# A two-part fp32 product: the context's high and low parts side by side in one 512-column matmul

## The chip, the cores and the metric

The kernel runs on one core of a Trainium2 chip, in one launch. The metric is its device time in microseconds, the median of repeated runs. Before the change three runs gave 1920.5, 1927.2 and 1932.17 us, so a median of 1927.2.

## The reference, cut to what matters

Two layers work on 512 latent tokens and 256 context tokens of width 1024. Layer 0 is grouped-query attention followed by a gated FFN of inner width 2816, layer 1 a bidirectional Mamba-2 (SSD) mixer followed by the same kind of FFN. The context passes through both mixers and the first FFN; only the latent stream is returned, so the second FFN has no context. All arithmetic is fp32.

```
for i in range(DEPTH):
    ...
    h_l = modulate(rms_norm(x, norm_mix_w[i]), mod_l[0], mod_l[1])
    h_c = modulate(rms_norm(ctx, norm_mix_w[i]), mod_c[0], mod_c[1])
    ...
    x = x + mod_l[2] * o_l
    if need_ctx_out:
        ctx = ctx + mod_c[2] * o_c
    h_l = modulate(rms_norm(x, norm_ffn_w[i]), mod_l[3], mod_l[4])
    x = x + mod_l[5] * conv_ffn(h_l, ffn_w_up[i], ffn_conv_w[i], ffn_conv_b[i], ffn_w_down[i])
    if need_ctx_out:
        h_c = modulate(rms_norm(ctx, norm_ffn_w[i]), mod_c[3], mod_c[4])
        ctx = ctx + mod_c[5] * conv_ffn(h_c, ffn_w_up[i], ffn_conv_w[i], ffn_conv_b[i], ffn_w_down[i])
```

`conv_ffn` splits `h @ w_up` into gate and value, convolves the gate over three neighbouring tokens, and multiplies `silu(gate) * value` by `w_down`.

## The kernel before

**Three products for one.** Activations lie transposed: channels on the 128 partitions, tokens along the free axis, 512 columns for the latent stream (L) and 256 for the context (C). TensorE takes a rounded fp32 format (fp32r), so every weight and every activation is split into a high part (a rounded copy, written by ACT) and a low part (the rest, a subtraction on DVE or POOL; `split`, line 81, and `modulated`, line 275). A product is three matmuls into one PSUM accumulation: high weights times high input (line 105), high weights times low input (106), low weights times high input (108). That is `mm3`, line 100. For the latent stream each of the three has 512 columns, for the context 256. Below, the three matmuls of one 128-row step for one stream are called a triple.

**Where the parts lie.** `htiles` (line 271) makes the high and the low tile of a stream separately, from a ring of 16 tiles per width. The FFN's hidden activations are split into two tiles of 768 columns (`hdh`, `hdl`, in `up`, line 841). The scratch ring t3 has 24 buffers of 768 columns during the first FFN.

**PSUM.** There are two buffers S of two banks (latents in columns 0 to 511, context in 512 to 767) and four buffers B of one bank.

**Layer 0, mixer.** `attention` (line 379) projects queries, keys and values. Context queries and keys come from six tiles `ps_c` and four tiles `ps_q`, eight triples each. The output projection runs in three groups of heads through `down` (`project`, line 1304, and the last group directly); its inputs are split in `osplit`.

**FFN.** `up` makes one 128-channel hidden tile: a gate tile and a value tile (`gemm_in`, line 351, eight steps, first 24 matmuls for one stream, then 24 for the other), ACT and DVE read the gate tile for the convolution and SiLU, DVE multiplies by the value tile and splits the result. There are 22 hidden tiles. After every two of them, `flush` runs `down` (line 779): for each of eight output tiles m it multiplies the two pending hidden tiles by `w_down` into a bank per stream, and DVE adds each bank, times a gate vector, into the residual (line 797). During the first FFN, DVE also computes the second layer's modulation in 96 pieces (`ada_dve`, line 154, instruction `junk`), taken from a generator a piece at a time between the tiles.

**Changeovers.** The last flush of a stage runs one segment after another: the context, then two halves of the latents. The norm of a segment runs beside the next segment's products. `first_tiles` (line 368) then makes the first two tiles of the next stage, starting with the context and the first half of the latents while the second half is still being normed.

**Layer 1, mixer.** `ssd` (line 889) makes a tile for the time steps (dt), and for each of eight groups two x tiles, one B tile, one C tile and two z tiles; x and B have both streams. `conv` (line 964) copies a tile out of PSUM with ACT into a row with gaps, then ACT and DVE run a five-tap convolution over it. The eight groups' states and outputs follow in `core`, one group behind. At the end the latent residual is loaded back from DRAM into `xn`, two tiles of 256 columns per m, and leaves at the end of the kernel in the same pieces.

**What sets the order.** The kernel is written for a planner that orders each engine's instructions at compile time: program order gives the priority, an instruction goes where its engine is free and its inputs are ready by the planner's own timing, and the planner assigns buffers as they fall free. So matmuls of a later tile can stand between those of an earlier one. Only the first part of `attention` fixes the order by hand for TensorE, ACT and DVE. On the chip each engine follows its list. Weights come through one DMA queue (SP) into tiles of 1024 columns (10 buffers) and are split by ACT and DVE (lines 85 and 87).

## Time and profile before

| | |
|---|---|
| median of three runs | 1927.2 us |
| runs | 1920.5, 1927.2, 1932.17 us |
| span of the profiled execution | 1929.7 us, mean granted clock of TensorE 0.990 |
| attention and output projection, about | 0 to 440 us |
| first FFN, about | 440 to 1000 us |
| SSD mixer, about | 1000 to 1550 us |
| second FFN, about | 1550 to 1930 us |

The profile is of one execution by the hardware profiler, and its own time is the span, from the first to the last instruction. It is 2.5 us above the median and within the range of the three runs. PE is TensorE's matmul, PEld its weight load, DVE VectorE, ACT ScalarE, POOL GpSimd, SP the engine that issues the DMAs. A row of the groups view names the kernel's line, the engine, the operation, what is written from what, the shape and the count; then the busy time in us, the mean length of one in ns, and the idle time before with what ended it. A row of the timeline gives the start in us, the length in us, and, in brackets, the idle time before it. A matmul's length includes its way through the pipeline, so two neighbours overlap, and what one costs is the distance from its start to the next one's. Some matmul records are missing, a few per cent at most.

### The profile page before, as it was taken

Reading aid. Unit: us, or ns where it says so; the run is one execution under the profiler, and the core shown is the slowest. Engines: PE = TensorE matmul, PEld = TensorE weight load, DVE = VectorE, ACT = ScalarE, POOL = GpSimd, SP = SyncE. Lnnn points to the kernel's source line nnn. Section 1 sums busy time; section 2 is a strip of 40 time slices with the busy share of each in tenths; the row PEclk is TensorE's granted clock in tenths of the full one; section 3 lists DMA queues with packets and bytes.
Section 4 is the critical chain, followed back from the end, with each engine's and each line's share of the span. In section 5 each row is a group of like instructions: output and inputs, shape, how many; then the busy total and the mean of one; then the engine's idle time right before and its main releaser. Section 6 shows DMA issues by size and latency. Waiting matters only on the chain.

```text
span 1929.7 us, 27392 instructions
## 1 busy us (share of the span) xinstructions
PE 1877.4 (97%) x10744; PEld 1533.9 (79%) x10744; DVE 1337.2 (69%) x1976; ACT 844.2 (44%) x1446; POOL 312.5 (16%) x274
## 2 busy tenths in 40 slices
PE   8989999999999999999999999999999999999999
PEld 6755544678888888888888888888888878888887
DVE  5577777768777777775577777777878466555555
ACT  3655444345222222222256777766677343333331
POOL 2241101022000000000031334443335210000000
PEclk9989998999999999999999999999999999999999
DMA  8221343104434443332222444344343322323332
GB/s 334 77 88 37 124 150 128 45 23 143 128 123 131 131 131 122 121 95 62 68 92 63 132 117 124 110 131 120 106 136 120 99 77 88 109 88 101 97 99 87
DMA packets 73424, 210.00 MB, mean 109 GB/s; under 512 B 8912, under 2 KB 14416, under 8 KB 73168
## 3 DMA queue, kind: packets, MB, share of 16 engines
q1 hardware_dynamic: 73296, 208.26, 34.0%
q8 instruction: 84, 1.38, 0.3%
q14 instruction: 44, 0.36, 0.1%
HBM read 198.79 MB, written 6.82 MB: 107 GB/s over the span
## 4 chain that ended last, share of the span: by engine, by line
PE 77%; DVE 8%; ACT 4%; issue 3%; POOL 2%; DMA 2%; SPq 0%; POOLq 0%; DVEq 0%; ACTq 0%
PE ps_up L108 10%; PE ps_up L106 10%; PE ps_up L105 10%; PE ps_d L105 6%; PE ps_d L106 6%; PE ps_d L108 6%; PE ps_in L108 4%; PE ps_in L106 4%; PE ps_in L105 4%; PE ps_o L650 2%; PE ps_s L686 2%; PE ps_st L1043 2%; PE ps_wo L108 1%; DVE ht L281 1%; PE ps_wo L105 1%
## 5 line engine op out<-in xcount | busy, mean ns | idle before, releaser
L87 DVE TENSOR_TENSOR wl<-wst,wh 128x1024 fp32r<-128x1024 f32 x205 | 255.4, 1246 | 222.8 <-PE ps_up L106 110.1
L85 ACT CAST wh<-wst 128x1024 fp32r<-128x1024 f32 x211 | 221.2, 1049 | 411.7 <-DMA wst<-in_wup 336.6
L106 PE MATMUL ps_up<-hlf,wh 128*128 128x512 f32 x1008 | 357.1, 354 | 0.0
L105 PE MATMUL ps_up<-hhf,wh 128*128 128x512 f32 x1008 | 356.9, 354 | 0.0
L108 PE MATMUL ps_up<-hhf,wl 128*128 128x512 f32 x1008 | 356.8, 354 | 0.0
L106 PEld LDWEIGHTS ps_up<-hlf,wh 128*128 128x128 f32 x1008 | 190.6, 189 | 26.2
L105 PEld LDWEIGHTS ps_up<-hhf,wh 128*128 128x128 f32 x1008 | 190.6, 189 | 26.2
L108 PEld LDWEIGHTS ps_up<-hhf,wl 128*128 128x128 f32 x1008 | 190.5, 189 | 25.9
L105 PE MATMUL ps_in<-hhs,wh 128*128 128x512 f32 (+1 forms) x560 | 204.4, 365 | 0.0
L106 PE MATMUL ps_in<-hls,wh 128*128 128x512 f32 (+1 forms) x560 | 199.4, 356 | 0.0
L108 PE MATMUL ps_in<-hhs,wl 128*128 128x512 f32 (+1 forms) x560 | 198.7, 355 | 0.0
L105 PE MATMUL ps_d<-hdh,wh 128*128 128x512 f32 (+1 forms) x568 | 193.7, 343 | 1.4 <-DVE X L797 1.2
L108 PE MATMUL ps_d<-hdh,wl 128*128 128x512 f32 (+1 forms) x568 | 193.4, 341 | 0.0
L106 PE MATMUL ps_d<-hdl,wh 128*128 128x512 f32 (+1 forms) x568 | 192.9, 340 | 0.3 <-DVE hdl L87 0.3
L797 DVE SCALAR_TENSOR_TENSOR X<-ps_d,mod,X 128x512 f32<-128x512 f32 (+1 forms) x240 | 132.9, 588 | 20.8 <-PE ps_d L108 20.4
L106 PEld LDWEIGHTS ps_d<-hdl,wh 128*128 128x128 f32 x568 | 106.7, 188 | 15.5 <-DVE hdl L87 0.7
L105 PEld LDWEIGHTS ps_d<-hdh,wh 128*128 128x128 f32 x568 | 106.3, 188 | 15.4 <-DVE X L797 1.7
L105 PEld LDWEIGHTS ps_in<-hhs,wh 128*128 128x128 f32 x560 | 105.9, 189 | 15.1 <-issue 1.2
L167 DVE SCALAR_TENSOR_TENSOR junk<-wada,cb 128x1024 f32<-128x1024 f32 x96 | 117.2, 1220 | 1.1 <-ACT cb L159 0.9
L108 PEld LDWEIGHTS ps_in<-hhs,wl 128*128 128x128 f32 x560 | 105.8, 189 | 14.7
L108 PEld LDWEIGHTS ps_d<-hdh,wl 128*128 128x128 f32 x568 | 106.7, 188 | 13.3
L106 PEld LDWEIGHTS ps_in<-hls,wh 128*128 128x128 f32 x560 | 106.0, 189 | 13.2
(344 smaller groups left out, 3525.0 us busy)
## 6 DMA issues: line engine op xcount, KB each, us to landing
wst<-in_wup SPq DMA_DIRECT2D x88, 512.0 KB, 3.6
wada<-in_adaT SPq DMA_DIRECT2D x48, 512.0 KB, 3.6
wst<-in_win SPq DMA_DIRECT2D x48, 512.0 KB, 3.6
wst<-in_wdown SPq DMA_DIRECT2D x44, 512.0 KB, 4.2
wada<-in_adaB SPq DMA_DIRECT2D x32, 512.0 KB, 5.2
E<-ad SPq DMA_DIRECT2D x64, 256.0 KB, 7.3
ec<-ead SPq DMA_DIRECT2D x64, 128.0 KB, 5.1
wst<-in_wout SPq DMA_DIRECT2D x16, 512.0 KB, 3.5
```

Of the source, the lines that this page charges most:

```text
L85: keep(nc.scalar.copy(hi, src))
L87: keep(eng.tensor_tensor(lo, src, _r(hi), ALU.subtract))
L105: mm(out, wh, ah, start=first, stop=False)
L106: mm(out, wh, al, start=False, stop=False)
L108: mm(out, wl, ah, start=False, stop=last)
L167: g.tc.keep_in_program_order(nc.vector.scalar_tensor_tensor(junk, w, 1.0, cb[:, v * D : (v + 1) * D], ALU.mult, ALU.mult, accum_out=md[:, ...
L281: nc.vector.scalar_tensor_tensor(t[:, c0:c1], ap, g.moda[layer][ca][:, m, v : v + 1], rs[:, c0:c1], ALU.mult, ALU.mult)
L650: nc.tensor.matmul(po[S64[e], :n], v, pr[:, 512 * e + off : 512 * e + off + n], start=first, stop=last)
L686: nc.tensor.matmul(outs[e], a[S64[e], k], b[S64[e], q], start=i == 0, stop=False)
L797: nc.vector.scalar_tensor_tensor(ap, o[:, c0:c1], gate[:, m, v : v + 1], ap, ALU.mult, ALU.add)
L1043: nc.tensor.matmul(ps[:, d * 256 : (d + 1) * 256], Bt[:, t * P : (t + 1) * P], xw[d][t], start=t == ts[0], stop=t == ts[-1])
```

## The change

The context's high and low parts move into one tile of two rows of 256 columns. One matmul of 512 columns multiplies both by the high weights, into a full bank: columns 0 to 255 hold high times high, 256 to 511 high times low. A second matmul of 256 columns adds the low weights times the high part to the first half. The latent triples stay as they are, except that the last step runs them in reverse order; where a group starts and stops in the same step with two halves, three narrow matmuls are kept. The two halves are added after the last step, in one of three ways:

- `fold`: ACT copies the second half to SBUF, DVE adds it into the first half in PSUM (up tiles of the FFN, the first tiles of a stage; of the SSD's two first tiles only the dt tile)
- `summed`: ACT copies the first half to its SBUF place, as before, and DVE adds the second half there (`ps_c`, `ps_q`, the x and B tiles of the SSD)
- in `down` the residual update on DVE runs once per half

The low and high hidden parts of the first FFN get tiles of two rows of 768 (`hd2`, six of them), and its scratch ring has 12 buffers instead of 24. `xn` becomes one tile of 512 columns per m, so its loads and the final stores are 8 transfers instead of 16.

```
     wh, wl = w
     mm = g.nc.tensor.matmul
-    for out, (ah, al) in outs:
-        mm(out, wh, ah, start=first, stop=False)
-        mm(out, wh, al, start=False, stop=False)
-    for out, (ah, al) in outs:
-        mm(out, wl, ah, start=False, stop=last)
+    for out, a in outs:
+        if len(a) == 3:
+            parts = [(out.rearrange("p (s n) -> p s n", s=2), wh, a[2]), (out[:, :C], wl, a[0])]
+        else:
+            parts = [(out, wh, a[0]), (out, wh, a[1]), (out, wl, a[0])]
+        if first and last and len(a) == 3:
+            mm(out[:, C:], wh, a[1], start=True, stop=True)
+            parts[0] = (out[:, :C], wh, a[0])
+        elif last:
+            parts.reverse()
+        for i, (o, s, mv) in enumerate(parts):
+            mm(o, s, mv, start=first and i == 0, stop=last and i == len(parts) - 1)
+
+
+def both(t):
+
+    return t[:, 0, L:], t[:, 1, L:], t[:, :, L:]
+
+
+def fold(g, ps):
+
+    t = t3(g, "fold", n=C)
+    g.nc.scalar.copy(t, ps[:, C : 2 * C])
+    g.nc.vector.tensor_tensor(ps[:, :C], ps[:, :C], t, ALU.add)
+
+
+def summed(g, out, ps):
+
+    g.nc.scalar.copy(out, ps[:, :C])
+    g.nc.vector.tensor_tensor(out, out, ps[:, C : 2 * C], ALU.add)
...
 def htiles(g, n, name):
+    if n == C:
+        t = g.p.tile([P, 2, C], F32R, tag="h256", bufs=8, name=f"h{name}")
+        return t[:, 0], t[:, 1], t
     return tuple(g.p.tile([P, n], F32R, tag=f"h{n}", bufs=16, name=f"{p}{name}") for p in ("hh", "hl"))
...
+                if k == KT - 1 and folded:
+                    for i, a, b in run:
+                        if i:
+                            fold(g, ps[:, off[i] : off[i] + 2 * C])
                 yield
...
+    if len(norm.streams) > 1:
+        for ps, _ in tiles[:folds]:
+            fold(g, ps[:, L:])
     return [ps for ps, _ in tiles]
...
-            k_step(k, j, ps[:, :C], hc)
-        nc.scalar.copy(raw[j][:, L:], ps[:, :C])
+            k_step(k, j, ps, hc)
+        summed(g, raw[j][:, L:], ps)
...
-                    nc.vector.scalar_tensor_tensor(ap, o[:, c0:c1], gate[:, m, v : v + 1], ap, ALU.mult, ALU.add)
+                    for h in range(2 if i else 1):
+                        nc.vector.scalar_tensor_tensor(ap, o[:, h * C + c0 : h * C + c1], gate[:, m, v : v + 1], ap,
+                                                       ALU.mult, ALU.add)
...
-        hi, lo = t3(g, "hdh", F32R, n=tot), t3(g, "hdl", F32R, n=tot)
-        split(g, hd, hi, lo)
...
+        hl = g.t3p.tile([P, 2, tot], F32R, tag="hd2", bufs=6, name="hd2")
+        split(g, hd, hl[:, 0], hl[:, 1])
+        return [(hl[:, 0, :L], hl[:, 1, :L]), both(hl)]
...
-            nc.scalar.copy(raw[:, L + 4 : L + 4 + C], ps[:, L:T])
+            summed(g, raw[:, L + 4 : L + 4 + C], ps[:, L:])
...
-    xn = [[g.p.tile([P, C], F32, tag="h256", bufs=16, name=f"x{m}{i}") for i in range(2)] for m in range(KT)]
+    xn = [[g.p.tile([P, L], F32, tag="h256", bufs=8, name=f"x{m}")] for m in range(KT)]
     for m in range(KT):
-        for i in range(2):
-            nc.sync.dma_start(xn[m][i], xd[m * P : (m + 1) * P, i * C : (i + 1) * C])
+        nc.sync.dma_start(xn[m][0], xd[m * P : (m + 1) * P])
...
-    g.t3p, g.n3 = pool("pf", phf), 24
+    g.t3p, g.n3 = pool("pf", phf), 12
```

More of the change, by code (lines that the diff above doesn't have):

```diff
@@ L283, in modulated @@
     bias = g.mod[layer][cb][:, m, v : v + 1]
-    hi, lo = (h[:, a:b] for h in hl)
+    hi, lo = (h[:, a:b] for h in hl[:2])
     if pool:
@@ L348, in gen, with gemm_in @@
             yield
-def gemm_in(g, tiles, h, off, segs):
+def gemm_in(g, tiles, h, off, segs, folded=True):
     for run in segs:
@@ L365, in firsts, with first_tiles @@
     return [load_w(g, u) for u in units]
-def first_tiles(g, ws, norm, bg):
+def first_tiles(g, ws, norm, bg, folds=2):
     ends = ending(norm.streams)
     tiles = [(S(g, "ps_first"), w) for w in ws]
-    for _ in gemm_in(g, tiles, norm.h, (0, L), [ends[:-1], ends[-1:]]):
+    for _ in gemm_in(g, tiles, norm.h, (0, L), [ends[:-1], ends[-1:]], False):
         next(bg, None)
@@ L513, in values @@
                 w = tuple(w[:, (k % 4) * 256 : (k % 4 + 1) * 256] for w in wv[k // 4])
-                ah, al = (a[:, c0 : c0 + P] for a in h[k])
+                ah, al = (a[:, c0 : c0 + P] for a in h[k][:2])
                 for i, (s, mv) in enumerate(((ah, w[0]), (ah, w[1]), (al, w[0]))):
@@ L858, in up @@
             nc.vector.tensor_tensor(hd[:, a:b], cv[:, a:b], ps, ALU.mult)
-        hi, lo = t3(g, "hdh", F32R, n=tot), t3(g, "hdl", F32R, n=tot)
-        split(g, hd, hi, lo)
-        return [(hi[:, off[i] : off[i] + streams[i][0]], lo[:, off[i] : off[i] + streams[i][0]]) for i in range(ns)]
+        if ns == 1:
+            hi, lo = t3(g, "hdh", F32R, n=tot), t3(g, "hdl", F32R, n=tot)
+            split(g, hd, hi, lo)
+            return [(hi, lo)]
+        hl = g.t3p.tile([P, 2, tot], F32R, tag="hd2", bufs=6, name="hd2")
+        split(g, hd, hl[:, 0], hl[:, 1])
+        return [(hl[:, 0, :L], hl[:, 1, :L]), both(hl)]
     gate = g.mod[layer][5]
@@ L894, in ssd @@
     h = norm.h
-    ps_dt, ps_x0 = first_tiles(g, wf, norm, bg)
+    ps_dt, ps_x0 = first_tiles(g, wf, norm, bg, 1)
     ph = ExitStack()
@@ L911, in gemm @@
         ps = S(g, "ps_in")
-        for _ in gemm_in(g, [(ps, w)], h, (0, L), [[(i, 0, (L, C)[i])] for i in streams]):
+        for _ in gemm_in(g, [(ps, w)], h, (0, L), [[(i, 0, (L, C)[i])] for i in streams], False):
             pass
```

17 lines of the change are left out of this document (11 added, 6 removed).

## The prediction

> **What bounds the kernel now.** I read the page first, for the engine with the least idle time and for the chain that ends last.
>
> ```profile
> span 1929.7 us, 27392 instructions
> ...
> PE 1877.4 (97%) x10744; PEld 1533.9 (79%) x10744; DVE 1337.2 (69%) x1976; ACT 844.2 (44%) x1446; POOL 312.5 (16%) x274
> ...
> PE 77%; DVE 8%; ACT 4%; issue 3%; POOL 2%; DMA 2%; SPq 0%; POOLq 0%; DVEq 0%; ACTq 0%
> ```
>
> TensorE is at work for 97% of the span and carries 77% of the chain. An average hides stages, so I asked for windows of 50 us (columns: PE, weight loads, DVE, ACT, POOL busy with counts, clock, DMA): two of the first FFN, with and without the second layer's modulation running beside it, and one of the SSD layer.
>
> ```profile
> 550.00:600.00 50.00, 50.00 (x291) 44.12 (x290) 37.57 (x59) 11.33 (x13) 0.00 (x0) 1.00 0.40 127
> 850.00:900.00 50.00, 50.00 (x291) 44.12 (x290) 30.71 (x48) 11.32 (x12) 0.00 (x0) 1.00 0.21 64
> 1150.00:1200.00 50.00, 49.77 (x304) 43.32 (x304) 36.22 (x43) 35.74 (x80) 22.43 (x19) 1.00 0.37 109
> ```
>
> In the long stages PE never pauses, at a full clock. A matmul taken off PE there shortens the span; work added on DVE costs nothing until DVE, at 37.57 of 50, runs out or holds up a PSUM buffer.
>
> **What a product costs on PE.** Durations of matmuls overlap, so I take the distance from start to start in the timeline. First a tile of the up projection (24 context products from 618.13, then 24 latent ones from 621.00), then a stretch of the down projection with six wide and six narrow products in turn.
>
> ```profile
> 618.13 0.28 PE L105 MATMUL ps_up<-hhf,wh 128*128 128x256 f32 x1
> 621.00 0.40 PE L105 MATMUL ps_up<-hhf,wh 128*128 128x512 f32 x1
> 621.24 0.40 PE L106 MATMUL ps_up<-hlf,wh 128*128 128x512 f32 x1
> 626.47 0.28 PE L105 MATMUL ps_up<-hhf,wh 128*128 128x256 f32 x1
> ...
> 600.17 0.39 PE L105 MATMUL ps_d<-hdh,wh 128*128 128x512 f32 x1
> 601.54 0.28 PE L105 MATMUL ps_d<-hdh,wh 128*128 128x256 f32 x1
> 602.22 0.39 PE L105 MATMUL ps_d<-hdh,wh 128*128 128x512 f32 x1
> ```
>
> Up: 24 narrow products take 2.87 us, 0.120 each; 24 wide ones 5.47 us, 0.228 each. Down: six narrow ones take 0.68 us, 0.113 each, six wide ones 1.37 us, 0.228 each. So a wide product costs hardly more or less than two narrow ones (0.240 or 0.227): **the change removes no columns**. A context triple streams 3 x 256 columns before and 512 + 256 after. What can go is only the 6 to 7 ns by which a narrow product in a long run of narrow ones is dearer than one among wide ones.
>
> **Part 1, PE.** An up triple costs 3 x 0.120 = 0.360 us now (2.87/8 = 0.359). Afterwards narrow and wide alternate one by one, which the trace does not show; the nearest is six and six, whose pair costs 2.05/6 = 0.342. With the narrow one staying at 0.120 the pair is 0.348. The worst bound comes from the wide product right behind a run of narrow ones, 621.00 to 621.24, 0.24 us: pair 0.36, no gain. I take 0.342 to 0.348, nearest to the six and six, so 12 to 17 ns per triple. The triples, by group (a group's mean there is its pipelined length, not its cost):
>
> ```profile
> L108 PE MATMUL ps_up<-hhf,wl 128*128 128x256 f32 x336 | 95.1, 283 | 0.0
> L105 PE MATMUL ps_in<-hhs,wh 128*128 128x256 f32 x184 | 55.3, 300 | 0.0
> L105 PE MATMUL ps_d<-hhoc,wh 128*128 128x256 f32 x64 | 18.6, 298 | 0.6 <-ACT hhoc L85 0.5
> ```
>
> 336 in up, 184 in the SSD projection, 64 in the output projection, and by the code 32 in the first tiles of the two stages (four tiles of eight steps): 616. These stand in long narrow runs, so each gives 12 to 17 ns: 7.4 to 10.5 us. The 176 context triples of the FFN's down projection already cost 3 x 0.113 = 0.340, so they give nothing, and the 80 of the attention stage (ps_c, ps_q) stand among waits and count as nothing. **Gain: 9.5 us**, the upper half because the six-and-six row is the nearest.
>
> A page of the Trainium skill speaks against even this. "TensorE: Matmul & The Clock Gate", section "Back-to-back issue gap", gives 262 cycles for 256 columns and 518 for 512, at 2.4 GHz. By it a triple would fall from 786 to 780 cycles, 2.5 ns, and all 872 triples would be worth 2.2 us, an estimate from that page alone. The trace's 0.120 in narrow runs and 0.113 among wide products, both at granted clock 1.00, do not fit one fixed cost per product.
>
> **Part 2, DVE and ACT.** Each halved result must be added up. The rows nearest to the new work are a residual update of 256 columns, a DVE tensor add or multiply with a PSUM operand of 256 columns, and ACT's copy of 256 columns out of PSUM.
>
> ```profile
> L797 DVE SCALAR_TENSOR_TENSOR X<-ps_d,mod,X 128x256 f32<-128x256 f32 x144 | 68.2, 479 | 10.4 <-PE ps_d L108 10.2
> L661 DVE TENSOR_TENSOR o<-ps_oc,y 128x256 f32<-128x256 f32 x8 | 3.4, 422 | 4.1 <-ACT y L660 4.1
> L970 ACT COPY raw<-ps_in 128x256 f32<-128x256 f32 x23 | 8.4, 364 | 0.0
> ```
>
> The residual takes two updates per context tile instead of one: 11 flushes and 3 output-projection groups of 8 tiles are 112 more, 112 x 0.479 = 54 us of DVE. A fold (ACT copies one half, DVE adds it into the other) stands in 44 up tiles and the dt tile; the variant that writes the sum to SBUF stands in 24 SSD tiles, 6 ps_c and 4 ps_q tiles, where ACT's copy exists already. That is 79 DVE adds, 79 x 0.422 = 33 us, and 45 ACT copies, 16 us. DVE goes from 1337 to about 1424 us. In the fullest FFN window, 50 us for two channel tiles, come 4 folds (1.7) and 8 updates (3.8): 37.6 becomes 43.1 of 50. That still fits.
>
> It has to fit in place too. In a flush (the down projection) DVE runs without a pause while it also does the modulation:
>
> ```profile
> 606.81 1.22 DVE L167 SCALAR_TENSOR_TENSOR junk<-wada,cb 128x1024 f32<-128x1024 f32 x1
> 607.95 1.15 DVE L797 SCALAR_TENSOR_TENSOR X<-ps_d,mod,X 128x512 f32<-128x512 f32 x2
> 609.00 1.23 DVE L167 SCALAR_TENSOR_TENSOR junk<-wada,cb 128x1024 f32<-128x1024 f32 x1
> ...
> 608.69 0.39 PE L106 MATMUL ps_up<-hlf,wh 128*128 128x512 f32 x1
> 608.92 0.39 PE L108 MATMUL ps_up<-hhf,wl 128*128 128x512 f32 x1
> ```
>
> One m tile takes DVE 609.00 - 606.81 = 2.19 us and PE 1.37 + 0.68 = 2.05, and the planner fills PE's difference with products of the next up tile (the two ps_up rows). One more update adds about 0.4 (the pair takes 1.05 from start to start, so the narrow one adds less than its 0.479). DVE then needs 2.6 against PE's 2.05: 0.55 x 8 = 4.4 us of filler per flush. The next up tile has 2.87 + 5.47 = 8.3 us of it. So I cost this at nothing; if that cover is missing, PE waits (second rival). A fold also delays the release of an up tile's PSUM pair by a copy, an add and whatever DVE does in between, 0.8 to 2 us; the pair is needed again only after the other tile's 8.3 us. Cost nothing there.
>
> **Part 3, where the new steps lie on the path.** Four places where PE waits for a chain that gets an added step, from the timeline (idle time and its releaser in brackets) and the waits (us in total, times, longest), and two DMA issues (KB, us to landing) for the end:
>
> ```profile
> 1051.83 0.92 PE L1154 MATMUL ps_end<-acsT,cst 128*128 128x192 f32 x4 [0.91 <-DVE acsT L1149]
> ...
> 90.86 0.42 PE L516 MATMUL ps_v<-wh,hha 128*128 128x256 f32 x1 [2.98 <-ACT raw L711]
> ...
> PE ps_first L106 <- POOL hls L288: 3.5, 3, 2.8
> ...
> PE ps_xt L1017 <- DVE xf L1120: 1.8, 6, 0.5
> ...
> xd<-X SPq DMA_DIRECT2D x8, 256.0 KB, 2.3
> ...
> out_dram<-x SPq DMA_DIRECT2D x16, 128.0 KB, 1.7
> ```
>
> At the start of the SSD layer DVE is the engine PE waits for; three sums (first two x tiles, B) of 0.422 join its queue ahead of acsT, 0 to 1.3 us, I take 1. The dt fold itself can run early, since the dt tile's context half is done before the latent one. In attention the last ps_c bank is freed by a DVE add after ACT's copy: 0.4 plus queueing, 0 to 1, I take 0.5. At the two changeovers into a first tile, the wide product needs both parts of the context input, where the old order could run on the high part; each context tile's second update also moves the norm later, and the scratch pool has 12 buffers instead of 24. 0 to 1 us each, I take 0.5 each, 1 together. In eight SSD groups the adds sit in DVE's queue before xf: 0 to 2 in all, I take 1. At the end the output leaves in 8 transfers of 256 KB instead of 16 of 128 KB: 2.3 - 1.7 = 0.6. The SSD output's x is loaded back in 8 transfers and added in one 512-wide step; PE is busy with the group's own work there, nothing. A reversed order of the three products at the last k changes no count. **Cost: 1 + 0.5 + 1 + 1 + 0.6 = 4.1 us**, bounds 0.6 and 5.9.
>
> **Sum.** The profiled span is 1929.7 and the median of the three runs 1927.2, 0.13% apart, so differences carry over as they are. 1929.7 - 9.5 + 4.1 = 1924.3 of span; against the median 1921.8, say **1922 us**, 0.3% less. A measurement of this kernel can tell about 0.5% from no change, 9.6 us: below 1917.6 counts as faster, above 1936.8 as slower. The likeliest case lies inside.
>
> **Rivals.** First, the full gain: the pair costs 0.340 to 0.342 as among wide products, all 616 triples give 17 to 18 ns (10.5 to 11), the attention triples add 80 x 0.017 = 1.4, and the adds hide: 1927.2 - 12 + 0.6 = **1916**. For it: PE's 50.00 of 50 with DVE free a quarter of the time. Against it: the PE waits quoted above exist and lie behind DVE.
>
> Second, slower: DVE becomes the pace of the flush. If the compile-time order puts no up products between the down tiles, each flush keeps PE waiting for PSUM banks for DVE's extra 8 x 0.4 = 3.2, and for two folds' 0.84. The modulation's 96 pieces last until about 860 us, where the DVE windows fall from 37.6 to 30.7, about eight flushes: 8 x 4.0 = 32 us, 1927.2 - 9.5 + 4.1 + 32 = **1954**. It decides once a flush gets under 2 us of filler; half missing gives 1938. For it: DVE is at 100% in a flush already. Against it: the order before holds exactly the filler needed, so the planner sees DVE's load.
>
> Third, no gain on PE: the pair costs 0.36, as the 0.24 of a wide product right behind narrow ones allows, and only the added steps remain: 1927.2 + 4.1 = **1931**. That is also the case in which the change doesn't do what it says, since 512 columns in one product take as long as 256 twice. For it: no columns go. Against it: the six-and-six row. By the Trainium skill's page named above this rival would be right but for 2.2 us.
>
> **How the numbers follow.** Forecast 1922 (1917 to 1927): 0.43. Full gain 1916: 0.25. No gain 1931: 0.20. DVE-paced flush 1938 and more: 0.12. Faster by over 0.5% is the full gain and the forecast's lowest edge, 0.25 + 0.04 = 0.29; slower is the second rival, 0.12; within 0.5% the rest, 0.59. The range leaves out the slower case and a little beyond the full gain: 1912 to 1934.
>
> **What would show each step.** In the changed profile 336 narrow up products should be left of 1008, with 336 more wide ones, and a tile's 16 alternating context products should take 8 x 0.342 to 0.348 = 2.74 to 2.78 us instead of 2.87; 2.87 or more makes the third rival right. DVE should show some 112 more updates and 79 adds, 43 of 50 in the 550 to 850 windows, with PE still at 50.00. PE rows in a flush that wait for DVE's update, or PE windows under 49.5 there, make the second rival right. The stage from 1026 to 1060 should grow by 1 us or so, the end by 0.6. If the span falls by more than 12 us, something beside the narrow runs was shortened, and my sum is wrong.

## The result, and the profile after

The changed kernel takes **1994.6 us** (median of 4 runs, 1992.9 to 1997.4) beside 1924.2 us for the kernel before (median of 4 runs, 1920.5 to 1932.2): 1.037 times the time before, 95% interval 1.034 to 1.040. That is 70 us slower; 1922 had been forecast, with 1934 as the upper end. The profiled execution has a span of 1995.6 us, 65.9 more than before. From the page of the changed kernel, the span, the busy times and the shares of the chain:

```profile
span 1995.6 us, 25761 instructions
...
PE 1896.9 (95%) x9880; PEld 1501.2 (75%) x9880; DVE 1407.0 (71%) x2080; ACT 856.7 (43%) x1491; POOL 301.7 (15%) x274
...
PE 72%; DVE 16%; issue 5%; ACT 4%; POOL 2%; DMA 1%; SPq 0%; DVEq 0%; POOLq 0%; ACTq 0%
```

DVE's busy time is what the forecast made it (1407 against 1424), and still only 71%. But its share of the chain has doubled, from 8% to 16%: it is hardly fuller, it is late. Where, the stages tell. Their lengths are taken from the timelines, from the first product of a stage to the first of the next one (the second FFN: to its last product):

| stage (us) | before | after | difference |
|---|---|---|---|
| up to the first ps_first (attention) | 432.1 | 436.4 | +4.3 |
| first FFN (first ps_up to the SSD layer's ps_first) | 530.8 | 550.6 | **+19.8** |
| SSD layer (first ps_in to first ps_wo) | 426.0 | 463.5 | **+37.5** |
| output projection (first ps_wo to the next ps_first) | 103.2 | 108.3 | +5.1 |
| three changeovers together | 76.2 | 74.7 | -1.5 |
| second FFN | 357.8 | 358.1 | +0.3 |

The attention stage is no finding: two other kernels below whose attention code is that of the kernel before show 421.0 and 431.7 us there. The other three lines are.

Next the waits of PE (us in total, times, longest) in the changed kernel:

```profile
PE ps_cb L1111 <- ACT Cf L1026: 26.6, 7, 4.6
PE ps_up L115 <- DVE wl L87: 12.3, 3, 4.7
PE ps_v L556 <- DVE raw L133: 5.2, 1, 5.2
PE ps_d L115 <- DVE X L841: 5.1, 9, 1.1
...
PE ps_y L1166 <- DVE E L1141: 3.0, 1, 3.0
```

The first row is the SSD layer, once per group from the second group on: 0.8 us, 2.9 us and then five times 4.6. The second row is the first FFN, and so are 1.9 us of the fourth. The two greatest have no counterpart in the waits before, where no row was over 6.3 us.

A pause can cost more than its length. Windows of the changed kernel (columns as in the prediction): two of the first FFN, one SSD group from ps_cb to ps_cb, the whole SSD stage, and the eight microseconds behind one pause at ps_up, which ended at 737.19:

```profile
550.00:600.00 50.00, 44.21 (x200) 35.34 (x199) 38.36 (x64) 11.28 (x14) 0.00 (x0) 0.97 0.39 127
850.00:900.00 50.00, 50.00 (x243) 41.94 (x242) 38.57 (x65) 12.61 (x16) 0.00 (x0) 1.00 0.26 87
1324.00:1385.60 61.60, 56.93 (x303) 47.69 (x303) 43.54 (x51) 37.82 (x83) 20.34 (x19) 0.97 0.35 103
1049.00:1513.00 464.00, 434.04 (x2311) 363.23 (x2312) 344.51 (x404) 292.10 (x621) 147.30 (x136) 0.97 0.40 113
737.00:741.00 4.00, 3.81 (x10) 3.00 (x11) 2.81 (x6) 1.59 (x2) 0.00 (x0) 0.58 0.98 384
741.00:745.00 4.00, 4.00 (x21) 3.33 (x20) 2.45 (x2) 1.35 (x2) 0.00 (x0) 0.99 0.29 120
```

And the same SSD group, and the whole stage, in the kernel before:

```profile
1284.50:1340.00 55.50, 55.00 (x327) 47.51 (x326) 41.99 (x49) 37.86 (x83) 22.77 (x20) 1.00 0.40 115
1027.00:1453.00 426.00, 423.22 (x2495) 366.40 (x2495) 326.23 (x379) 294.29 (x622) 154.89 (x135) 1.00 0.41 120
```

For almost four microseconds behind the pause PE has 0.58 of its clock: 10 products start where later 21 do, at a cost of 4 x 0.42 = 1.7 us. In the SSD stage PE is idle for 30.0 us instead of 2.8, and busy for 10.8 us longer although it issues 184 matmuls fewer: 27.2 + 10.8 = 38.0, the whole loss. Some 9 of the 10.8 are the clock. It stands at half behind each of the five pauses of 4.6 us, three times for 3.4 us of PE's work and twice for about 4.3, so an estimate is 0.5 x (3 x 3.4 + 2 x 4.3) = 9.4; and in ssd_nosel below, whose stage keeps a clock of 1.00, PE is busy for 8.5 us less than here. In the FFN the three pauses give 12.3, the low clock behind them 3 x 1.7 = 5.1 and the waits for X 1.9, together about 19, less a gain on the products of two or three; some 3 of the 19.8 us remain unexplained.

The Trainium skill's page "TensorE: Matmul & The Clock Gate", section "What's actually happening", states that PE falls to half its clock after at least one idle window of about 3.4 us and comes back after about as long a busy one. The rows agree with the half clock and with its length: 0.58 and then 0.99, behind a pause of 3.8 us. They do not agree with the 3.4 us of idleness as a limit: waits of about 2 us lost the clock too in other runs, as the last section shows.

So the question is why PE pauses at these two places while DVE is idle for 18 us of each SSD group. First the FFN. VectorE's timeline in the changed kernel, at the end of a flush:

```profile
728.01 1.71 DVE L841 SCALAR_TENSOR_TENSOR X<-ps_d,mod,X 128x256 f32<-128x256 f32 x3
729.64 1.22 DVE L197 SCALAR_TENSOR_TENSOR junk<-wada,cb 128x1024 f32<-128x1024 f32 x1
...
733.38 0.43 DVE L127 TENSOR_TENSOR ps_up<-ps_up,fold 128x256 f32<-128x256 f32 x1 [2.12 <-ACT fold L126]
733.72 0.47 DVE L841 SCALAR_TENSOR_TENSOR X<-ps_d,mod,X 128x256 f32<-128x256 f32 x1
734.12 1.22 DVE L197 SCALAR_TENSOR_TENSOR junk<-wada,cb 128x1024 f32<-128x1024 f32 x1
...
735.92 1.22 DVE L87 TENSOR_TENSOR wl<-wst,wh 128x1024 fp32r<-128x1024 f32 x1
```

DVE works through the flush in order: three residual updates and one modulation filler per output tile. Then it stands still for 2.12 us before a fold that waits for ScalarE's copy, and the split of the next up tile's weights (wl) is queued behind that fold, one more update and one more filler. PE starts the next tile at 737.19, when wl is there.

In an SSD group ps_cb needs Cf, the output of C's convolution. ScalarE's timeline of the changed kernel, ahead of the pause that ends at 1385.56:

```profile
1368.44 0.59 ACT L1017 COPY raw<-ps_in 128x512 f32<-128x512 f32 x1 [1.92 <-PE ps_in L115]
...
1376.28 0.63 ACT L1173 ACTIVATE ysq<-z 128x512 f32<-128x512 f32 x1 [2.70 <-DVE z L1171]
1376.81 0.80 ACT L1020 ACTIVATE Cf<-raw,par 128x512 f32<-128x512 f32 x1
...
1384.88 0.63 ACT L1026 ACTIVATE Cf<-Cf 128x512 f32<-128x512 f32 x1 [5.57 <-DVE Cf L1022]
```

The same steps in the kernel before, where PE came to ps_cb at 1340.05 and didn't wait:

```profile
1332.21 0.63 ACT L1124 ACTIVATE ysq<-z 128x512 f32<-128x512 f32 x1 [1.14 <-DVE z L1122]
1332.75 0.81 ACT L971 ACTIVATE Cf<-raw,par 128x512 f32<-128x512 f32 x1
...
1339.11 0.63 ACT L977 ACTIVATE Cf<-Cf 128x512 f32<-128x512 f32 x1 [2.74 <-DVE Cf L973]
```

In both, Cf's first step stands in ScalarE's queue behind ysq, the last piece of the previous group's y, which comes through VectorE. Before, ysq began 7.8 us ahead of the moment at which PE was ready for ps_cb (1340.05), and Cf was done 0.3 us ahead of it. After, PE's last ps_in product starts at 1380.58, so PE would be ready at about 1380.8: ysq begins only 4.5 us ahead of that, 3.3 us later than before. And the way from Cf's first step to the last one's start is 8.07 us instead of 6.36. Those 3.3 and 1.7 use up the 0.3 that was spare and make the pause of 4.6. PE's order has moved too: before, the previous group's second pair of y products ran behind C's tile (1323.21 to 1326.11, while C's copy began at 1323.41), and in the changed kernel it runs ahead of that tile (ps_y from 1361.37, C's copy at 1368.44), so that PE is ready sooner after C's tile.

### The profile page after: what moved, and what is told of

It reads as the page before. It is cut to its first block, busy times and chain, and to the rows that moved or that the text cites. A ratio compares the mean times of both kernels' runs of the same rounds, so it can differ in the third digit from the quotient of the medians.

```text
span 1995.6 us, 25761 instructions
## 1 busy us (share of the span) xinstructions
PE 1896.9 (95%) x9880; PEld 1501.2 (75%) x9880; DVE 1407.0 (71%) x2080; ACT 856.7 (43%) x1491; POOL 301.7 (15%) x274
## 4 chain that ended last, share of the span: by engine, by line
PE 72%; DVE 16%; issue 5%; ACT 4%; POOL 2%; DMA 1%; SPq 0%; DVEq 0%; POOLq 0%; ACTq 0%
PE ps_up L115 29%; PE ps_d L115 16%; PE ps_in L115 7%; PE ps_wo L115 4%; PE ps_o L693 2%; PE ps_s L729 2%; PE ps_st L1092 2%; DVE xf L1022 2%; PE ps_q L115 2%; DVE ht L314 1%; DVE Cf L1022 1%; DVE wl L87 1%; PE ps_l L115 1%; DVE X L841 1%; DVE Bf L1022 1%
## 5 line engine op out<-in xcount | busy, mean ns | idle before, releaser
L115 PE MATMUL ps_up<-hhf,wl 128*128 128x512 f32 x672 | 251.0, 393 | 12.3 <-DVE wl L87 12.3
L115 PE MATMUL ps_up<-hhf,wh 128*128 128x512 f32 x672 | 259.3, 393 | 0.0
L841 DVE SCALAR_TENSOR_TENSOR X<-ps_d,mod,X 128x256 f32<-128x256 f32 (+1 forms) x352 | 178.6, 549 | 15.0 <-PE ps_d L115 14.0
L115 PE MATMUL ps_d<-hd,wh 128*128 128x512 f32 (+1 forms) x576 | 165.5, 374 | 3.2 <-DVE X L841 3.0
L115 PE MATMUL ps_in<-hhs,wh 128*128 128x512 f32 x376 | 147.5, 395 | 0.6 <-DVE raw L133 0.6
L115 PE MATMUL ps_in<-hls,wh 128*128 128x512 f32 x376 | 146.7, 390 | 0.0
L115 PE MATMUL ps_in<-hhs,wl 128*128 128x512 f32 x376 | 140.0, 393 | 0.4
L115 PE MATMUL ps_up<-hf,wh 128*128 128x512 f32 x336 | 121.9, 397 | 0.0
L115 PEld LDWEIGHTS ps_d<-hd,wh 128*128 128x128 f32 x576 | 99.8, 188 | 20.3 <-DVE X L841 4.8
L115 PE MATMUL ps_d<-hd,wl 128*128 128x256 f32 (+1 forms) x376 | 94.5, 325 | 0.6 <-ACT hd L85 0.5
```

The source lines that it names most:

```text
L115: mm(o, s, mv, start=first and i == 0, stop=last and i == len(parts) - 1)
L841: nc.vector.scalar_tensor_tensor(ap, o[:, h * C + c0 : h * C + c1], gate[:, m, v : v + 1], ap, ALU.mult, ALU.add)
```

## The experiments

Each kernel ran on one chip beside the kernel before, and its ratio is to that. Fifteen kernels ran. Lines beginning with - and + are against the changed kernel unless it says otherwise.

**1. The SSD products back to narrow (ssd_narrow).** In gemm for ps_in the context takes three 256-column products again; the conversion is a copy. The two first tiles keep the wide product and are both folded.

```diff
-    ps_dt, ps_x0 = first_tiles(g, wf, norm, bg, 1)
+    ps_dt, ps_x0 = first_tiles(g, wf, norm, bg)
...
-            summed(g, raw[:, L + 4 : L + 4 + C], ps[:, L:])
+            nc.scalar.copy(raw[:, L + 4 : L + 4 + C], ps[:, L:T])
```

> The change is undone in the SSD stage's in-projection alone: the context parts of ps_in take the three 256-column products again and their conversion is one ScalarE copy, with no add; the FFN and the attention keep the change. Theory (the 37.5 us lost in the SSD stage are a PE pause before ps_cb in each group, made by the add that now stands in the chain to Cf, and the half clock behind the pause): no pause at ps_cb, the stage from the first ps_in to the first ps_wo is 426 +- 2 us again (463.5 after, 426.0 before), the total 1957 +- 4 us. Rival (the loss comes from what is not undone here: the two-part layout of the tiles, the rings, the eight wide reload tiles): the stage stays at 455 us or more, the total above 1985 us.

1976.0 us, ratio 1.026 (1.022 to 1.030); the stage is 448.9 us. Neither theory had that. The waits at ps_cb are down to 2.7 us in six, but a new row leads in this stage:

```profile
PE ps_xt L1066 <- DVE xf L1169: 14.0, 7, 2.9
```

Undoing the products and adds in this stage takes back 14.6 of 37.5 us. The engines' order in it, written at compile time, is not that of the kernel before again, and VectorE is now 2 us late at another place.

**2. The SSD products wide, without the add (ssd_noadd).** The same edit of the conversion, with the wide products kept.

> The SSD stage keeps the wide products, but the add of the second half is left out in its convolutions, so the context's low part is missing there. Theory (the VectorE add, not the product, makes the loss): the stage is 423 to 426 us, the total 1954 to 1958 us. Rival (the wide product itself, its whole PSUM bank or its slower instruction costs the time): the pause at ps_cb stays and the stage is 455 us or more.

1952.5 us, ratio 1.015 (1.011 to 1.018); the stage is 430.0 us, four more than expected, and far from the rival's 455. The three adds per group (412 ns each in the changed kernel, 24 x 0.41 = 10 us of VectorE's time) thus make 33.5 of the 37.5 us, together with the new order that comes with them; the wide product and its full bank are not the cause.

**3. Is it the add's place in the chain? (ssd_side, ssd_load)** In both the conversion is the plain copy, and an add of the same size follows whose result nobody reads. In ssd_side it reads the PSUM tile, in ssd_load only SBUF.

```diff
-            summed(g, raw[:, L + 4 : L + 4 + C], ps[:, L:])
+            nc.scalar.copy(raw[:, L + 4 : L + 4 + C], ps[:, L:T])
+            t = t2("half")[:, :C]
+            nc.vector.tensor_tensor(t, raw[:, L + 4 : L + 4 + C], ps[:, T : T + C], ALU.add)
```

> The change, but in the SSD convolutions the VectorE add of the second half writes to a tile that nobody reads, so that it loads VectorE and holds the PSUM bank as before and is no step on the way to xf and Bf; the context's low part is missing there. Theory (place in the chain: the add delays B's chain and the compile-time order puts the previous group's y products ahead of C's tile, which takes away what covered the chain to ps_cb): no wait at ps_cb; VectorE's 1.2 us more per group can make ps_xt late instead, so the stage is 430 to 450 us (463.5 after, 430.0 without the add). Rival (VectorE's time or the held PSUM bank makes the loss wherever the add's result goes): 458 us or more.

> As ssd_side (no add on the way to xf and Bf), but the idle VectorE add reads SBUF only, so that the PSUM tile is free as soon as ScalarE has copied it. Theory (three more instructions in VectorE's queue, 1.2 us a group, are enough, through the order): the stage is 455 to 470 us as in ssd_side (468.6). Rival (the PSUM tile held until VectorE has read it delays the in-projection and the order): 430 to 436 us as with no add at all.

ssd_side: 2001.1 us, ratio 1.040 (1.039 to 1.042), stage 468.6. ssd_load: 2005.6 us, ratio 1.042 (1.038 to 1.046), stage 476.5. My theory of ssd_side fell: an add that is no step on any chain costs more than the one in the change (463.5). So did the rival of ssd_load, whose stage lies 6.5 us above even its theory's range: no held PSUM tile is needed. The waits have moved; in ssd_side they are

```profile
PE ps_yo L1159 <- DVE hs L1104: 16.3, 9, 2.1
...
PE ps_in L115 <- DVE wl L87: 7.4, 4, 2.0
```

**4. Does it need the wide products? (b_load)** The kernel before, untouched but for the idle add of ssd_load.

> The kernel before, all its narrow products kept, with one idle VectorE add of 256 columns from SBUF to SBUF behind each of a group's three context conversions (24 in all, about 10 us of VectorE's time in 426). Theory (the stage has no slack for three more instructions in VectorE's queue, whatever the products are): PE waits appear at ps_xt, ps_cb or ps_yo and the stage is 445 to 475 us. Rival (the loss needs the wide products too, whose pairs end earlier): 426 to 432 us.

1982.0 us, ratio 1.030 (1.026 to 1.033); the stage is 475.7 us, 49.6 more than before, just above what the theory expected. Three instructions that compute nothing, 10 us of VectorE in 426, cost 50 us of a stage in which VectorE was idle for 100. PE's waits for it:

```profile
PE ps_cb L1064 <- ACT Cf L979: 9.7, 4, 3.9
PE ps_yo L1110 <- DVE hs L1055: 8.9, 8, 2.1
PE ps_xt L1019 <- DVE xf L1122: 7.6, 4, 2.1
```

**5. Does it need added work at all? (b_order)** The kernel before with not one instruction added: the previous group's second pair of y products is emitted ahead of C's tile instead of behind it, against the kernel before:

```diff
             if G is None:
-                next(prev, None)
+                nb += 1
+                for _ in range(2 if nb == 1 else 0):
+                    next(prev, None)
                 continue
```

> The kernel before, with no product, tile or add changed: in each SSD group the previous group's second pair of y products (ps_yo, ps_y) is emitted before C's tile instead of behind it, which is where the changed kernel's engines have it. Theory (the order of the work around C's tile, with no slack left for VectorE's and ScalarE's queues, makes the loss, and the adds only led the planner to it): PE waits of some us per group, the stage 440 to 465 us (426.0 before). Rival (the loss needs the three adds' work on VectorE): 426 to 431 us.

1940.0 us, ratio 1.008 (1.005 to 1.010); the stage is 440.3 us, at the theory's lower edge. Order alone costs 14.3 us, through one wait of about 2 us a group:

```profile
PE ps_bt L1024 <- ACT Bf L977: 12.0, 7, 2.0
```

**6. Two orders for the changed kernel (ssd_swap, ssd_late).** All work kept. ssd_swap makes C's tile ahead of B's; ssd_late has b_order's edit with nb == 2, which emits both pairs of y products behind C's tile. The edit of ssd_swap:

```diff
-        for name, i, st in (("B", 2, (1, 0)), ("C", 3, (0,))):
+        for name, i, st in (("C", 3, (0,)), ("B", 2, (1, 0))):
```

> The change with one edit: each SSD group makes C's tile ahead of B's, so that C's conversion has more of PE's work behind it before ps_cb needs it. All work is kept, the three adds included. Theory (the pause is a lack of cover behind C's chain, 17.5 us long with 12.6 us of other products behind it): no wait for Cf at ps_cb, the stage 426 to 445 us (some of it may come back where B's chain is now the late one). Rival (the adds load VectorE too much in whatever order): 458 us or more.

> The change with all its work, adds included, but the previous group's y products are emitted behind C's tile instead of one pair ahead of it and one behind. Theory (the order decides: more of PE's work behind C's tile hides its chain): no wait for Cf at ps_cb, the stage 430 to 450 us (463.5 after). Rival (three adds in VectorE's queue cost what they cost in any order): 455 us or more.

ssd_swap: 1968.1 us, ratio 1.023 (1.021 to 1.025), stage 442.9, the wait for Cf gone and a smaller one at ps_bt (8.2 us in seven) in its place. ssd_late: 2006.2 us, ratio 1.043 (1.038 to 1.047), stage 480.1, the wait for Cf worse:

```profile
PE ps_cb L1111 <- ACT Cf L1026: 37.9, 7, 7.9
```

The theory of "cover behind C's tile" falls with ssd_late: there the y products gave PE more to do behind C's tile, and Cf came later still, because its steps stood behind the y work in VectorE's and ScalarE's queues, as in the changed kernel, and that work now came later. With ssd_swap they stand ahead of the second half of it. So what stands in front of Cf in those queues counts, and more work for PE meanwhile is not enough. (ssd_swap also puts B's products behind C's tile, so it does not separate the two.)

**7. The add taken off VectorE (ssd_pooladd).** ScalarE copies both halves, GpSimd adds them in SBUF.

```diff
-            summed(g, raw[:, L + 4 : L + 4 + C], ps[:, L:])
+            t = t2("half", n=512)[:, :C]
+            nc.scalar.copy(raw[:, L + 4 : L + 4 + C], ps[:, L:T])
+            nc.scalar.copy(t, ps[:, T : T + C])
+            nc.gpsimd.tensor_tensor(raw[:, L + 4 : L + 4 + C], raw[:, L + 4 : L + 4 + C], t, ALU.add)
```

> The change with all its work, but the SSD convolutions' second half is copied to SBUF by ScalarE and added there by GpSimd, so VectorE has no add and the PSUM tile is free after ScalarE's copies; the chain is longer by a copy and GpSimd's start. Theory (VectorE's queue is what is late): the stage is 428 to 442 us. Rival (the length of the chain from the product to xf and Bf): 455 us or more.

2012.8 us, ratio 1.045 (1.041 to 1.050); the stage is 488.6 us, the worst of all. VectorE's own load is not the measure either: the same sum made by ScalarE and GpSimd in these chains costs more still.

**8. What makes Cf's own steps slower (ssd_nosel).** Cf's way is 1.7 us longer after the change. VectorE's timeline of the changed kernel there, its four taps among the products xw:

```profile
1377.65 1.24 DVE L1022 SCALAR_TENSOR_TENSOR Cf<-raw,par,Cf 128x512 f32<-128x512 f32 x1 [0.81 <-ACT Cf L1020]
...
1379.85 1.12 DVE L1022 SCALAR_TENSOR_TENSOR Cf<-raw,par,Cf 128x512 f32<-128x512 f32 x1
...
1382.20 1.11 DVE L1022 SCALAR_TENSOR_TENSOR Cf<-raw,par,Cf 128x512 f32<-128x512 f32 x1
...
1384.10 0.74 DVE L1022 SCALAR_TENSOR_TENSOR Cf<-raw,par,Cf 128x512 f32<-128x512 f32 x1
```

and GpSimd's in the same time:

```profile
1378.29 4.48 POOL L1125 TENSOR_SCALAR_AFFINE_SELECT E<-E 128x512 f32<-128x512 f32 x4
```

The second and the third tap (1.12 and 1.11) run while GpSimd masks E, and the last one, behind the masks, takes 0.74. The first one's 1.24 lies mostly beside another GpSimd instruction, the sum of ysq, which ends at 1378.34. The products xw between the taps are slow with the masks as well: 1.12 and 1.38, where those beside no mask took 0.68 and 0.94. Before, three of the four taps there took 0.74, since the masks came behind them:

```profile
1338.71 3.45 POOL L1076 TENSOR_SCALAR_AFFINE_SELECT E<-E 128x512 f32<-128x512 f32 x2 [4.24 <-DMA E<-ad]
```

The edit leaves the masks out:

```diff
-                nc.gpsimd.affine_select(c4(e), c4(e), ...)
...
-AF.Exp, bias=nacs[:, c, row : row + 1]
+AF.Exp, scale=0.0, bias=acsT[:, c, row : row + 1]
```

> The change, with GpSimd's 64 masks of E (affine_select) left out, and E's exponential taken of a column alone so that it stays finite; E's values and so the output of the SSD layer are others. VectorE's instructions around Cf stand in the same order as in the changed kernel. Theory (GpSimd's masks beside Cf's taps slow VectorE there, 1.1 to 1.25 us a tap instead of 0.74, and so make some 2 of the 4.6 us of each pause at ps_cb): the wait there is 2 to 3 us and the stage 445 to 453 us (463.5 after). Rival (what is late is Cf's first step behind the y chain, the masks don't matter): the wait stays at 4 us or more and the stage at 458 us or more.

1967.4 us, ratio 1.021 (1.018 to 1.023); the stage is 436.8 us, better than the theory expected, with all three adds in place. The taps of Cf (duration in ns: least, median, greatest) in the changed kernel:

```profile
L1022 DVE SCALAR_TENSOR_TENSOR Cf<-raw,par,Cf x32: 735/1116/1419, 1076.5 to 1506.7; 128x512 f32<-128x512 f32 x32
```

The same line in this kernel:

```profile
L1022 DVE SCALAR_TENSOR_TENSOR Cf<-raw,par,Cf x32: 735/741/1250, 1068.1 to 1473.7; 128x512 f32<-128x512 f32 x32
```

And PE's wait for Cf in it:

```profile
PE ps_cb L1111 <- ACT Cf L1026: 10.1, 7, 1.8
```

The wait at ps_cb falls from 26.6 us to 10.1, and with pauses of up to 1.8 us in place of 4.6 the clock of the stage is back at 1.00. Cf's way from its first step to the last one's start takes 6.44 us instead of 8.07. That is how masks that slow a group's taps, and the products between them, by 1.6 us come to be worth 26.7 us of the stage. (On PE some y products stand a little later than in the changed kernel, so that not quite all of it need be theirs. The first tap still takes 1.24 us, beside the sum of ysq.)

**9. The first FFN: three single cuts (ffn_one, ffn_pool, ffn_nofill).** ffn_one drops the second residual, ffn_pool makes the up weights' wl on GpSimd, ffn_nofill moves the modulation filler out of the flush:

```diff
-                    for h in range(2 if i else 1):
+                    for h in range(1):
```
```diff
-            w = load_w(g, I["wup"][layer, t])
+            w = load_w(g, I["wup"][layer, t], lo_engine="dve" if layer else "pool")
```
```diff
-            next(side, None)
...
-        next(side, None)
+        for _ in range(3):
+            next(side, None)
         pu = gemm(NFT + f)
-        next(side, None)
+        for _ in range(2):
+            next(side, None)
```

> The change with the second residual of the context left out in the first FFN's down product (its low part times the high weights is missing there): 112 VectorE instructions fewer. Theory (the flush's queue on VectorE, above all the added residuals, delays wl): all three pauses go, the stage is 527 to 532 us, the total 1973 to 1978 us. Rival (the fold's add, which waits for ScalarE's copy ahead of wl, is enough by itself): two pauses of about 4.2 us with a half clock behind each stay, the stage is 538 to 543 us.

> The change with one edit: in the first FFN the low parts of the up weights are made on GpSimd instead of VectorE. Theory (the three PE pauses of 4.2 to 5.1 us in the first FFN come from wl standing in VectorE's queue behind the flush's second residuals and the fold's add): no pause at ps_up, the stage from the first ps_up to the first product of the next stage is 527 to 531 us (550.6 after, 530.8 before), the total 1973 to 1977 us. Rival (VectorE has too much work in the flush whatever the order): PE's waits for X in the flush stay and the stage is 538 us or more.

> The change with all its work, but the modulation filler on VectorE (96 instructions of 1.2 us) no longer runs one to each output tile of the first FFN's flush; it runs between the up tiles, five to a pair. Theory (my second rival: the flush is paced by VectorE, whose three residuals and one filler take 2.6 us a tile where PE needs 2.1): no PE waits for X or wl in the flush, the first FFN 527 to 532 us (550.6 after). Rival (the fold ahead of wl in VectorE's queue makes the pauses): 538 us or more.

ffn_one: 1968.8 us, ratio 1.023 (1.020 to 1.026), FFN 528.7, no pause left and 2.1 us less than before: the 42 folds cost nothing by themselves. ffn_pool: 1986.0 us, ratio 1.032 (1.029 to 1.036), FFN 540.8: the pauses at ps_up are gone, and PE waits for the residuals instead, 11.0 us in all where the changed kernel had 5.1 (7.0 and 1.9 of them in the first FFN). The theory (527 to 531) falls and the rival, too much work on VectorE in the flush, stands:

```profile
PE ps_d L115 <- DVE X L841: 11.0, 13, 1.1
```

ffn_nofill: 1980.0 us, ratio 1.028 (1.024 to 1.032), FFN 537.2, between the two: the pauses at ps_up are gone with all the work kept, and one of 5.2 us is left where the first flush waits for its own wl. Without that pause and the low clock behind it the stage would be at about 530, an estimate. So the flush has too much on VectorE, as my second rival said: three residuals and a filler, 2.6 us a tile. wl behind it in the queue is the form that the lateness takes.

**10. The change only where it hides (up_pair, up_group).** The kernel before with wide products and folds only in the first FFN's up tiles: alternating wide and narrow (up_pair), or seven wide, eight narrow, one wide (up_group):

```diff
+GROUP = [(k, j) for k in range(7) for j in (0, 1)] + [(7, 1), (7, 0)]
```
```diff
+GROUP = [(k, 0) for k in range(7)] + [(k, 1) for k in range(KT_)] + [(7, 0)]
```

> The kernel before, with the wide product and the fold only in the first FFN's up tiles (42 tiles of eight k-steps, 336 pairs); everywhere else the three narrow products. Each pair alternates a 512- and a 256-column product. Theory (a pair costs 0.352 us on TensorE where three narrow products took 0.359; the loss came from the added steps elsewhere): no pauses, the first FFN 2 to 3 us shorter than before's 530.8, the SSD stage 426 +- 1, the total 1920 to 1923 us beside 1924. Rival (the fold's two added instructions per tile stop PE by themselves): the first FFN is 534 us or more.

> As up_pair, but a tile's eight 512-column products stand together and its eight 256-column products stand together (seven wide, eight narrow, the last wide). Theory that the width's change from product to product costs the missing part of my forecast's gain (234.6 + 117.2 ns alternating, 227 + 113 ns in runs of one width): a pair takes 0.340 to 0.343 us, the first FFN is 5 to 6 us shorter than before's, the total 1917 to 1920 us. Rival (a pair's price doesn't hang on its order): the first FFN as in up_pair, within 1 us.

up_pair: 1925.9 us, ratio 1.0008 (0.9991 to 1.0024). up_group: 1922.7 us, ratio 0.9991 (0.9972 to 1.0009). Neither can be told from the kernel before. Their first FFNs are 529.9 and 528.5 us beside 530.8; the SSD stages 425.8 both, without a pause. A tile's context products in up_group:

```profile
610.58 1.75 PE L375 MATMUL ps_up<-hf,wh 128*128 128x512 f32 x7
612.17 1.11 PE L375 MATMUL ps_up<-hf,wl 128*128 128x256 f32 x8
613.12 0.40 PE L375 MATMUL ps_up<-hf,wh 128*128 128x512 f32 x1
613.35 0.40 PE L105 MATMUL ps_up<-hhf,wh 128*128 128x512 f32 x1
```

Eight pairs take 613.35 - 610.58 = 2.77 us, 0.346 each. Both theories had expected more. Both kernels gained some 1.5 to 2 us less in the first FFN than 336 pairs at these prices should give (336 x 0.0075 = 2.5 and 336 x 0.013 = 4.4 us); where that is left stays open.

## Why the prediction was wrong

**The pair's price, Part 1.** I took 0.342 to 0.348 us for a pair and 9.5 us for all. The changed kernel's up tile, from its first context product to the first latent one:

```profile
630.49 0.39 PE L115 MATMUL ps_up<-hf,wh 128*128 128x512 f32 x1
630.72 0.28 PE L115 MATMUL ps_up<-hf,wl 128*128 128x256 f32 x1
...
633.30 0.40 PE L115 MATMUL ps_up<-hhf,wh 128*128 128x512 f32 x1
```

2.81 us for eight pairs, 0.351 each: between the forecast's 2.74 to 2.78 and the third rival's 2.87. The step that failed was the choice of the six-and-six row for products that alternate one by one. up_group, where products of one width stand together, comes to 2.77. At 0.359 - 0.351 = 8 ns the 616 triples were worth 5 us, half of the forecast. It is the lesser error.

**The flush costs nothing, Part 2.** "So I cost this at nothing; if that cover is missing, PE waits (second rival)": this step failed. The sum per tile was right: 2.6 us of VectorE against 2.05 of PE, and the windows from 550 to 850 have DVE near the 43 of 50 (38.4 to 41.1). The planner did put up products between the down tiles, so I looked for cover in the right place. But I counted only PE's filler and not what lies behind the flush in VectorE's own queue: the wl without which PE has no next tile to fill with. My sign for the second rival, PE windows under 49.5 there, is the first row of the windows above, 44.21. Its place and engine were right, its price (4 us in each of eight flushes) and its point of decision were not: three flushes paid about 6 us each, the others little. ffn_one shows it: without the second residual the stage gains the 2.1 us that the pairs give.

**"In eight SSD groups the adds sit in DVE's queue before xf: 0 to 2 in all, I take 1."** This is the step that cost most, 37.5 us. I had quoted the row that warned of it, six waits of PE for xf of up to 0.5 us, and read the small total as slack. It meant the opposite: in those six groups VectorE reached that point only just after the moment in which PE needed it. The path was wrong as well: in the changed kernel no row has PE waiting for xf, and the loss stands at ps_cb, where PE waits 26.6 us for Cf, a place that I had not listed. I priced three adds at their length, as if the rest stayed where it was. But the order of every engine's work is laid down at compile time from all the instructions, and b_load shows what three idle ones a group do to this stage: +49.6 us. b_order shows that a new order alone, with no work added, gives +14.3. And the low clock behind the pauses I had not priced at all: some 9 of the 38 us.

A sum in Part 3 is also wrong: by its own terms the upper bound of the cost is 1.3 + 1 + 2 + 2 + 0.6 = 6.9, not 5.9. The forecast does not hang on it.

What did not fail: PE's 0.3 us more from the SSD stage's first product to its first ps_cb (38.1 beside 37.9, forecast 1 with a lower bound of 0); the changeovers (no loss, forecast 1); the end (0.3 us, forecast 0.6); the counts (352 updates of X for 240, 42 folds in the up tiles and the other adds). The wait at ps_v grew from 3.0 to 5.2, beyond the 0 to 1 that I allowed; but b_load, whose attention code is that of the kernel before, has 5.5 there, so the growth need not be the change's.

The output projection's 5.1 us lie with the last SSD group's y products, which run in it: the wait for E in the waits above (3.0 us) lies there, and the stage is 101.7 us in ssd_noadd.

What stays open: how much of the SSD loss is the added instructions themselves and how much the order that the planner makes of them, since none of my edits added the instructions and kept the order. Shown is that a new order without added work is enough for a loss, that idle instructions are, and that with the masks gone from beside Cf's taps most of it goes.

## What to carry to other kernels

A stage in which PE is at 99% and every engine else has idle time can still have no slack: look for short waits that recur in each round at the same place, and test it by adding an instruction that does nothing (here 10 us of idle work cost 50). Before merging products to save 8 ns each, ask where the sum of the halves goes; it is free only where its queue has nothing urgent behind it, as in the up tiles. And price a pause of PE with the low clock that can follow it: here 1.7 us and more behind each long one, and sometimes behind a wait of 2 us too.

## What the runs showed of the hardware

In the changed kernel each pause of PE of 3.8 to 4.7 us in the two long stages is followed by half the clock for 3.4 us or somewhat more of its work (0.58 in the window behind 737), worth 1.7 us or more. For shorter waits the length does not tell: those of up to 2.0 us, one a group in b_order, left the stage at a clock of 1.00, as those of up to 1.8 us did in ssd_nosel, and behind the wait of 2.9 us at ps_cb (which ended at 1203.03) the changed kernel has 1.00 as well. But waits no longer than these did lose it elsewhere. In ssd_narrow, windows behind two waits at ps_xt, of 2.15 and of 2.06 us:

```profile
1252.70:1256.70 4.00, 4.00 (x22) 3.37 (x23) 2.49 (x4) 2.72 (x5) 1.30 (x1) 1.00 0.00 0
1310.40:1314.40 4.00, 3.98 (x15) 3.48 (x16) 2.54 (x4) 2.79 (x6) 1.27 (x1) 0.60 0.00 0
```

In b_load, behind a wait of 1.78 us at ps_xt:

```profile
1106.70:1110.70 4.00, 3.96 (x14) 3.24 (x15) 2.60 (x4) 2.73 (x5) 1.28 (x1) 0.59 1.00 322
```

What decides between them stays open.

VectorE's taps of 512 columns, which read two SBUF operands, took 1.11 and 1.12 us while GpSimd masked E, 1.24 beside its sum of ysq, and 0.74 else; a mask took 4.48/4 = 1.12 us in that time. The Trainium skill's page "SBUF — State Buffer", section "SBUF: two separate sides", says that a VectorE operation with two SBUF inputs and a GpSimd operation that reads SBUF share a port pair that one of them holds for a whole instruction. The runs agree as far as they go: without the masks the median tap is 0.741 us instead of 1.116. On a chain with no slack the masks were worth most of the loss.

In up_group's rows a 256-column product costs 0.119 us in a run of its own width (612.17 to 613.12 for eight) and a 512-column one 0.227 (610.58 to 612.17 for seven), 0.346 together; when they alternate one by one, a pair took 0.351.
